# The gate of an mLSTM layer kernel: transposing the normed tokens by VectorE and DRAM instead of TensorE, with the norm's gain in the weights

## The chip, the core and the metric

The kernel runs on one core of a Trainium2 chip, on one layer's worth of work for 2048 tokens of width 1024. The metric is the device time of one execution in microseconds. Engines are named as in the profile: PE (TensorE), DVE (VectorE), ACT (ScalarE), POOL (GpSimd), SP (SyncE, which only issues DMAs here).

## What is computed

One layer: an mLSTM mixer, a squared-ReLU MLP, and then a last part, the only one that the change touches:

```python
h = h + mlstm_mixer(rmsnorm(h, norm_mix), ...)
h = h + sqrelu_mlp(rmsnorm(h, norm_mlp), w1, w2)
gate = jax.nn.sigmoid(rmsnorm(h, norm_ple) @ ple_gate_w + ple_gate_b)   # 1024 x 1024
h = h + gate * (p @ ple_w)                                            # p: 2048 x 256
return rmsnorm(h, norm_final)
```

`rmsnorm(x, g)` is `x * rsqrt(mean(x^2) + eps) * g`, all in float32.

## The kernel before

Products are made on TensorE with both operands split into a high and a low part (`split`, L165: an ACT cast to the high part, a DVE subtract for the low one), so that each product takes three matmuls (`mm3`). A matmul contracts over partitions, so the activations have to stand with their 1024 features on partitions: they are transposed before each product.

**The down projection** of the MLP is a sequence of jobs (`down`, 48 of them). Each ends in 512 KB stores `h_d<-o` (L1287) that POOL issues and that add to the residual stream in DRAM (`h1_d`). Other work is hung on jobs as `side` lists; the table `late` (L1636) hangs the loads and splits of the last part's weights on jobs 41 to 47: eight 128x1024 slices of the gate's weights (`wgt`), two of `ple_w` (`wpl`).

**The last part** takes 16 token tiles of 128 (class `Tok`, loop from L1648). For a tile: `load` brings the 512 KB of `h2` to SBUF; `norm` squares and sums on ACT, makes `r = rsqrt(...)` in a few tiny steps (`rstd`), and multiplies `h2` by `r` and by the broadcast row `row_ple` on DVE into `xs`; `tr0` and `tr1` transpose four 128x128 blocks each on TensorE into the one PSUM bank that `ps_s` gives for `pt`, and `split` reads that bank; `half(0)` and `half(1)` each do 24 matmuls into `pg` (`gate`) and 6 into `pl` (`p @ ple_w`, with `p` transposed earlier), then DVE adds the bias (`g<-pg`), ACT takes the sigmoid, DVE multiplies with `pl` and adds to `h`; `fin` applies the final norm and POOL stores the tile (`out<-h`). The steps of a tile are interleaved with those of its neighbours: while tile t is multiplied, tile t+1 is transposed and tile t+2 normed; `load` of tile t+4 is called in tile t.

Two helpers that were there before are used by the change. `shuffle` (L335) makes a transpose without TensorE: for one 256-feature slice `m` and four token tiles, DVE transposes 32x32 blocks (four `y<-raw` of 128x256), and POOL writes the result to DRAM in four 128 KB DMAs (L341) whose addresses put the blocks where the full transpose wants them. `shuffled` (L344) loads it back as `z`, 128 partitions by 2 x 512. Before, this is done for `p` (class `Early_p`) and in earlier stages.

Buffers come from tagged pools: `Ht` is the large pool of 4 KB rows, `Ot` has 7 buffers (`NO = 7`), used for the `o` tiles of the down projection and for `h2` from tile 2 on. What the program issues is put in its order on each engine by a scheduler, which follows the program's order but moves instructions by its estimates of time; every engine then takes its own queue in order.

Of the kernel before, what the change touches and what calls it, by code (L numbers as in the profile page):

```python
# [8 lines left out]
F32 = mybir.dt.float32  # L9
F32R = mybir.dt.float32r  # L10
AF = mybir.ActivationFunctionType
ALU = mybir.AluOpType
# [4 lines left out]
P = 128  # L17
S = 2048
D = 1024
KD = D // P  # L20
NC = S // P
# [14 lines left out]
def hybrid_mlstm_kernel(  # L36
# [100 lines left out]
    gains = {nm: const.tile([P, KD], F32, name=f"g_{nm}") for nm in ("mix", "hn")}  # L137

    def gain_load(nm, g):
        SP.dma_start(gains[nm], g.rearrange("(k p) -> p k", p=P))  # L140
# [9 lines left out]
    h1_d = dram.tile([NC, P, D], F32, name="h1_d")  # L150
# [18 lines left out]
    def rstd(ss, n):  # L169
# [9 lines left out]
        V.tensor_tensor(y, y, t, op=ALU.mult)  # L179
        return y  # L180

    def small(nm, bufs=3):
        return sb.tile([P, 8], F32, tag=nm, bufs=bufs, name=nm)
# [6 lines left out]
    class Weight:  # L190
# [11 lines left out]
                SP.dma_start(self.st[..., at:at + n], src)  # L202
                at += n

        def prep(self, eng=None):
            self.hi = Ht("whi", self.shape, F32R)
            self.lo = Ht("wlo", self.shape, F32R)
            split(self.hi, self.lo, self.st, eng)
            self.st = None

    def cols_w(w, c0, n=P):
# [2 lines left out]
    def rows_w(w, r0):  # L214
        return Weight(w[r0:r0 + P, :], [P, D])
# [119 lines left out]
    def shuffle(dst, m, srcs, tile_=Ht):  # L335

        y = tile_("y", [P, 8, 4, 32])
        for j in range(4):
            V.transpose(y[:, :, j, :], srcs[j].rearrange("p (b i) -> p b i", i=32))
        for q in range(4):  # L340
            G.dma_start(dst[8 * m:8 * m + 8, :, q].rearrange("b i e -> i b e"),  # L341
                        y[32 * q:32 * q + 32].rearrange("i b j t -> i b (j t)"))

    def shuffled(src, m, tile_=Ht):  # L344
        z = tile_("z", [P, 2, 512])
        SP.dma_start(z, src[8 * m:8 * m + 8].rearrange("(k b) i q e -> (b i) k (q e)", b=4))
        return z
# [4 lines left out]
    def by_quad(d, t):  # L352

        q = t % 4
        return d[t - q:t - q + 4, 32 * q:32 * q + 32]

    class Early(Prep):
# [575 lines left out]
    class Chunk:  # L933
        Cf = Cs = None

        ss, nss = None, H
# [370 lines left out]
    wgt = [rows_w(gate_w, k * P) for k in range(KD)]  # L1307
# [4 lines left out]
    def ple_rows(d, t):  # L1312
        return d[t] if t < NC // 2 else by_quad(d, t)

    class Early_p:
# [21 lines left out]
        def split(self):  # L1337
            self.hi, self.lo = Ht("pTh", [P, 2, 512], F32R), Ht("pTl", [P, 2, 512], F32R)
            split(self.hi, self.lo, self.z)

    class Tok:
        def __init__(self, t, pt):
            self.t, self.pt = t, pt

        def load(self):
            self.h2 = (Ht if self.t < 2 else Ot)("h2", [P, D])
            SP.dma_start(self.h2, ple_rows(h1_d, self.t))

        def norm(self):
            xs, ss = Ht("xs", [P, D]), small("ss1")  # L1350
            A.activation(xs, self.h2, AF.Square, scale=1.0 / 32.0, accum_out=ss[:, 0:1])
            r = rstd(ss[:, :1], 1)
            V.scalar_tensor_tensor(xs, self.h2, r[:, 0:1], rowc["ple"], op0=ALU.mult, op1=ALU.mult)
            self.xs = xs

        def tr(self, i):
            if i == 0:
                self.hi, self.lo = Ht("xTh", [P, KD, P], F32R), Ht("xTl", [P, KD, P], F32R)
            pt, ks = ps_s("pt"), slice(4 * i, 4 * i + 4)
            for k in range(4):  # L1360
                TE.transpose(pt[:, k * P:(k + 1) * P], self.xs[:, (4 * i + k) * P:(4 * i + k + 1) * P], ident)
# [10 lines left out]
        def half(self, n, gate=True):  # L1372

            if n == 0:
                self.ss = small("ssf")
            if gate:
                self.gate(n)
            sl, pg = slice(n * 512, (n + 1) * 512), self.pg
            tk = slice((self.t % 4) * P, (self.t % 4 + 1) * P)
            pl = ps_tr("pl")  # L1380
            for k in range(2):
                mm3(pl, self.pt.hi[:, k, tk], self.pt.lo[:, k, tk], wpl[k].hi[:, sl], wpl[k].lo[:, sl], k == 0, k == 1)
            g, h = St("g", [P, 512]), self.h2[:, sl]
# [91 lines left out]
    for n, pr in ((0, pa[0][0]), (2, pa[0][1])):  # L1475
        e = pr.early()
# [17 lines left out]
    t0, t1 = pa[0][0].trs(), pa[0][1].gets()  # L1494
# [121 lines left out]
    n = ENTER[-1] + NQ  # L1616
    down = [down_job(s % NQ, [pr for pr, e in zip(pairs, ENTER) if e <= s < e + NQ], (x0 if s % NQ < 4 else x1).rows)
            for s in range(n)]
# [10 lines left out]
        up[1][-1].side += pr.preps()  # L1629

    pp = [Early_p(t) for t in (0, 4, 8, 12)]
    toks = [Tok(t, pp[t // 4]) for t in range(NC)]
    for g in range(4):
        down[16 + 4 * g].side.append(pp[g].dma)
        down[18 + 4 * g].side.append(pp[g].put)
    late = {41: [wgt[0].dma, wgt[1].dma, lambda: row_load("ple", norm_ple[0])],  # L1636
            42: [wgt[0].prep, wgt[1].prep, wgt[2].dma, toks[0].load],
            43: [wgt[2].prep, wgt[3].dma, wgt[4].dma, toks[1].load, toks[0].norm],
            44: [wgt[3].prep, wgt[4].prep, wgt[5].dma, toks[2].load, lambda: row_load("gb", gate_b[0])],
            45: [wgt[5].prep, wgt[6].dma, wgt[7].dma, pp[0].get, toks[1].norm, toks[3].load],  # L1640
            46: [wgt[6].prep, wgt[7].prep, toks[0].tr0, pp[0].split],
            47: [wpl[0].dma, wpl[1].dma, toks[0].tr1, lambda: row_load("nf", norm_final)]}
    for s, fs in late.items():
        down[s].side += fs
    run7(up[0] + up[1] + down)


    for t in range(NC):  # L1648
        nx = toks[t + 1] if t + 1 < NC else None
        if nx:  # L1650
            nx.tr0()
        if t == 0:
            toks[t].gate(0)
            pg0 = toks[t].pg
# [11 lines left out]
        if t % 4 == 2 and t + 2 < NC:  # L1666
            pp[t // 4 + 1].split()
        if t % 4 == 0 and t + 4 < NC:
            pp[t // 4 + 1].get()
# [30 lines left out]
```

## Time and profile before

| | |
|---|---|
| Median of 3 runs | 2424.86 us (2423.91 to 2424.92) |
| The profiled execution | 2426.04 us, of which its span is 2424.3 us |
| TensorE busy in the span | 2375.9 us (98%) |
| VectorE, ScalarE, GpSimd busy | 65%, 48%, 25% |
| Start of the last part (first matmul into `pg`) | 2166.9 us |
| DMA share in 2150 to 2175, 2175 to 2200, 2200 to 2225 | 0.91, 0.68, 0.21 |

The span is what the trace covers; the profiled execution's own time is 1.74 us longer. In the rows of the profile, `out<-in` names the tiles that an instruction writes and reads, "L100" is a wrapper through which all engine calls go, so the names tell the groups apart. "Idle before" is the time that the engine stood still just ahead of these instructions, followed by what ended it. "SPq" and "POOLq" are the queues in which SP and POOL issue DMAs.

### The profile page before, as it was taken

The numbers are of one execution on the slowest core, as the hardware profiler recorded it, in microseconds if no ns is written. First come the engines' busy times: TensorE is split into PE (matmuls) and PEld (weight loads), VectorE is DVE, ScalarE is ACT, GpSimd is POOL, SyncE is SP. The second block draws the span as 40 slices with busy tenths as digits, with TensorE's granted clock in tenths as the row PEclk, the third lists the DMA queues.
The fourth block names the chain that finished last, engine by engine and source line by source line (L and its number), as shares of the span: only waits on it lengthen the run. The fifth ranks groups of instructions, "written<-read, shape, count | busy, mean of one in ns | idle before, by whom it ended". The sixth has DMA issues, their size and how long they took to land.

```text
span 2424.3 us, 31650 instructions
## 1 busy us (share of the span) xinstructions
PE 2375.9 (98%) x11317; PEld 1958.0 (81%) x11317; DVE 1573.3 (65%) x2601; ACT 1163.7 (48%) x2166; POOL 601.8 (25%) x633
## 2 busy tenths in 40 slices
PE   7999999999999999999999999999999999999998
PEld 6988888787889987888888888787887888887776
DVE  6667545557777887667674444866676767656665
ACT  5245424436788874433343333544443444445554
POOL 1041122124333324446543333011111111110000
PEclk9999999999999999999999999999999999999999
DMA  5676656867768873457573321667677776892211
GB/s 171 230 214 203 190 143 221 288 220 279 239 218 287 287 261 116 133 160 224 193 233 114 110 96 61 185 148 165 153 184 173 175 161 156 192 229 86 78 56 48
DMA packets 264501, 429.11 MB, mean 177 GB/s; under 512 B 46952, under 2 KB 174312, under 8 KB 264344
## 3 DMA queue, kind: packets, MB, share of 16 engines
q1 hardware_dynamic: 204376, 303.23, 38.2%
q0 software_dynamic: 59680, 123.35, 21.8%
q8 instruction: 88, 1.44, 0.2%
q14 instruction: 69, 0.57, 0.1%
q10 hardware_dynamic: 288, 0.52, 0.1%
HBM read 257.62 MB, written 169.21 MB: 176 GB/s over the span
## 4 chain that ended last, share of the span: by engine, by line
PE 77%; issue 8%; DVE 6%; DMA 4%; ACT 4%; POOL 1%; SPq 0%; DVEq 0%; ACTq 0%; POOLq 0%
PE pa L100 30%; PE pb L100 15%; PE pc L100 7%; PE psf L100 6%; PE pso L100 5%; PE pg L100 4%; PE psv L100 4%; PE pn L100 3%; PE pu L100 1%; PE pt L100 1%; PE pl L100 1%; ACT L100 1%; DMA hst<-hid_d 1%; DMA cb_d<-Clo 1%; DVE h L100 1%
## 5 line engine op out<-in xcount | busy, mean ns | idle before, releaser
L100 PE MATMUL pa<-op 128*128 128x512 f32 x3360 | 826.1, 395 | 6.6 <-ACT e L100 3.6
L100 PEld LDWEIGHTS pa<-op 128*128 128x128 f32 x3360 | 630.4, 188 | 159.0 <-ACT e L100 6.5
L100 PE MATMUL pb<-op 128*128 128x512 f32 x1632 | 407.8, 394 | 0.8 <-DVE op L100 0.8
L100 PEld LDWEIGHTS pb<-op 128*128 128x128 f32 x1632 | 306.2, 188 | 74.0 <-DVE op L100 1.1
L100 DVE TENSOR_TENSOR op<-sa,op 128x1024 fp32r<-128x1024 f32 (+2 forms) x176 | 188.7, 1078 | 147.4 <-ACT op L100 111.6
L100 ACT CAST op<-sa 128x1024 fp32r<-128x1024 f32 (+2 forms) x176 | 156.4, 895 | 167.6 <-PE pb L100 84.2
L1287 POOL DMA_DIRECT2D h_d<-o x96 | 93.1, 973 | 563.3 <-DVE o L100 494.1
L100 ACT COPY e<-pa 128x512 f32<-128x512 f32 x160 | 93.8, 587 | 262.1 <-PE pa L100 261.4
L100 PE MATMUL pc<-op 128*128 128x512 f32 x768 | 191.8, 394 | 0.1
L100 PEld LDWEIGHTS pc<-op 128*128 128x128 f32 x768 | 144.2, 188 | 34.5 <-DVE op L100 0.6
L100 PE MATMUL psv<-whi,xT 128*128 128x272 f32 (+2 forms) x720 | 161.7, 318 | 0.6 <-DVE xT L98 0.6
L100 PE MATMUL psf<-xT,whi 128*128 128x512 f32 x512 | 160.6, 394 | 0.0
L100 DVE TENSOR_TENSOR op<-wst,op 128x512 fp32r<-128x512 f32 x112 | 123.8, 1108 | 34.8 <-ACT op L100 22.0
L100 ACT CAST op<-wst 128x512 fp32r<-128x512 f32 x112 | 92.6, 834 | 108.5 <-DVE op L100 59.6
L100 PEld LDWEIGHTS psv<-whi,xT 128*128 128x128 f32 x720 | 118.9, 189 | 10.0 <-DVE xT L98 0.8
L461 POOL TENSOR_TENSOR sa<-wst 128x512 f32<-128x512 f32 x32 | 58.9, 1841 | 264.8 <-PE pb L100 168.5
L100 PE MATMUL psv<-wlo,xT 128*128 128x272 f32 (+2 forms) x360 | 114.1, 317 | 0.0
L100 PEld LDWEIGHTS psf<-xT,whi 128*128 128x128 f32 x512 | 95.2, 188 | 21.3
L100 PE MATMUL pso<-whi,hThi 128*128 128x512 f32 x256 | 102.1, 400 | 3.7 <-ACT nt L100 2.5
L100 PE MATMUL pg<-whi,xTl 128*128 128x512 f32 x256 | 101.9, 398 | 0.0
L100 PE MATMUL pg<-whi,xTh 128*128 128x512 f32 x256 | 101.1, 395 | 0.0
L100 PE MATMUL pg<-wlo,xTh 128*128 128x512 f32 x256 | 101.0, 394 | 0.0
(254 smaller groups left out, 4338.3 us busy)
## 6 DMA issues: line engine op xcount, KB each, us to landing
wst<-in_mlp_w SPq DMA_DIRECT2D x96, 512.0 KB
h_d<-o POOLq DMA_DIRECT2D x96, 512.0 KB, 12.4
hid_d<-e SPq DMA_DIRECT2D x128, 256.0 KB
hst<-hid_d SPq DMA_DIRECT2D x64, 384.0 KB
wst<-in_mlstm_w_in SPq DMA_DIRECT2D x44, 512.0 KB
vst<-v_d SPq DMA_DIRECT2D x31, 512.0 KB
raw<-in_x SPq DMA_DIRECT2D x16, 512.0 KB
kq<-kq_d SPq DMA_DIRECT2D x16, 512.0 KB
```

The lines of the kernel that those rows point to most:

```text
L100: r = f(*a, **kw)
L461: eng.tensor_tensor(s[:, 0], r1[:, :, P:], r2[:, :, P:], op=add_)
L1287: G.dma_start(rows(h1_d, 2 * q + i), o[i], accum_op=add_)
```

## The change

Four things are done.

- The gain `norm_ple` goes into the gate's weights: `prep` takes a gain per partition, ACT scales while it casts, DVE scales while it subtracts. The row `row_ple` is not loaded any more; a column version `g_ple` (128 x 8) is, by `gain_load`.
- The factor `r` of the norm is applied behind the matmul: `g = pg * r + gb` in one DVE instruction. `norm` now only makes `r`; nothing has to be normed before it is transposed.
- Tiles 0 to 3 transpose the raw `h2` on TensorE, as `xs` before.
- Tiles 4 to 15 are transposed by `shuffle` and `shuffled`, four tiles at a time (class `Early_h`): four more 512 KB loads of the same rows (`raw`, from the 7 buffers of `Ot`), 16 DVE transposes, 16 POOL stores of 128 KB, four `z` loads of 512 KB on SP. `STEPS` spreads this over the four tiles before. `tr` of these tiles is then a split of four 128x256 pieces from SBUF, with nothing on TensorE.

```diff
+    class Early_h:
+        def load(self):
+            self.raw = []
+            for j in range(4):
+                t = Ot("raw", [P, D])
+                SP.dma_start(t, by_quad(h1_d, self.t0 + j) if self.t0 < NC // 2 else h1_d[self.t0 + j])
+                self.raw.append(t)
+        def put(self, m):
+            shuffle(self.d, m, [r[:, m * 256:(m + 1) * 256] for r in self.raw])
+        def get(self, m):
+            self.z[m] = shuffled(self.d, m)
...
         def norm(self):
-            xs, ss = Ht("xs", [P, D]), small("ss1")
-            A.activation(xs, self.h2, AF.Square, scale=1.0 / 32.0, accum_out=ss[:, 0:1])
-            r = rstd(ss[:, :1], 1)
-            V.scalar_tensor_tensor(xs, self.h2, r[:, 0:1], rowc["ple"], op0=ALU.mult, op1=ALU.mult)
+            ss, self.r = small("ss1"), small("rt", 4)[:, 0:1]
+            A.activation(Ht("jn", [P, D]), self.h2, AF.Square, scale=1.0 / 32.0, accum_out=ss[:, 0:1])
+            rstd(ss[:, :1], 1, self.r)
...
         def tr(self, i):
+            if self.e:
+                tk = slice((self.t % 4) * P, (self.t % 4 + 1) * P)
+                for m in (2 * i, 2 * i + 1):
+                    split(self.hi[:, 2 * m:2 * m + 2], self.lo[:, 2 * m:2 * m + 2], self.e.z[m][:, :, tk])
+                return
...
-            V.tensor_tensor(g, pg, rowc["gb"][:, sl], op=ALU.add)
+            V.scalar_tensor_tensor(g, pg, self.r, rowc["gb"][:, sl], op0=ALU.mult, op1=ALU.add)
...
+    gp = [lambda k=k: wgt[k].prep(None, gains["ple"][:, k:k + 1]) for k in range(KD)]
-    late = {41: [wgt[0].dma, wgt[1].dma, lambda: row_load("ple", norm_ple[0])],
-            42: [wgt[0].prep, wgt[1].prep, wgt[2].dma, toks[0].load],
+    late = {41: [wgt[0].dma, wgt[1].dma],
+            42: [gp[0], gp[1], wgt[2].dma, toks[0].load],
...
+    down[30].side.append(lambda: gain_load("ple", norm_ple[0]))
+    STEPS = [[lambda e: e.load(), lambda e: e.put(0)], [lambda e, m=m: e.put(m) for m in (1, 2, 3)],
+             [lambda e, m=m: e.get(m) for m in range(4)], []]
...
+        g, i = t // 4 + 1, t % 4
...
+        if g < 4:
+            for f in STEPS[i]:
+                f(eh[g])
```

(`e` is None for tiles 0 to 3, so `tr` is there as before but reads `h2` instead of `xs`.)

The scheduler moves instructions by this. Three places matter for what follows. A row is an instruction with what it waits for: DMASW and DMAHW are DMAs issued by POOL and by SP or ACT; a name with _49 is that engine's or queue's semaphore.

On SP, where the down projection ends, before: loads of tiles 4 to 8 (`h_19155` and on), with a load of `p` among them.

```order
L1347 DMA h_19155<-h_d 128x1024 [waits DMASW7_49,DMAHW3_49,DMASW6_49,DMASW5_49]
L346 DMA z<-p_d 128x2x512 [waits DMAHW4_49,PE_49]
L1347 DMA h_19235<-h_d 128x1024 [waits DMAHW5_49,DMASW6_49,DMASW1_49]
L1347 DMA h_19358<-h_d 128x1024 [waits DMASW7_49,DMASW2_49]
L1347 DMA h_19485<-h_d 128x1024 [waits DMASW3_49,DMAHW7_49,DMASW0_49,DVE_49]
L1347 DMA h_19608<-h_d 128x1x1024 [waits DMASW4_49,DMAHW0_49,DMASW1_49,Activation_49]
L346 DMA z<-p_d 128x2x512 [waits DMAHW4_49,DMAHW1_49,DVE_49]
```

And after, from the load of tile 4 (`h_19158`) on, the same stretch of SP's queue:

```order
L1373 DMA h_19158<-h_d 128x1024 [waits DMASW7_49,DMAHW3_49,DMASW6_49,DMASW5_49]
L1358 DMA raw<-h_d 128x1x1024 [waits DMAHW4_49,DMASW6_49,DMASW1_49]
L1358 DMA raw<-h_d 128x1x1024 [waits DMAHW5_49,DMASW7_49,DMASW2_49]
L352 DMA z<-p_d 128x2x512 [waits PE_49]
L1358 DMA raw<-h_d 128x1x1024 [waits DMASW3_49,DMAHW7_49,DMASW0_49,DVE_49]
L1358 DMA raw<-h_d 128x1x1024 [waits DMASW4_49,DMAHW0_49,DMASW1_49,Activation_49]
L1373 DMA h_19255<-h_d 128x1024 [waits DMAHW4_49,DMAHW1_49,DVE_49]
L1373 DMA h_19405<-h_d 128x1024 [waits DMAHW5_49,DMAHW2_49,DVE_49]
L1373 DMA h_19537<-h_d 128x1024 [waits DMAHW7_49,DMAHW3_49,DVE_49]
```

The four `raw` loads of the first group stand where the loads of tiles 5 to 8 stood, with the same waits for POOL's stores (DMASW); tiles 5 to 8 come behind them. For the second group, SP's rows are

```order
L1358 DMA raw<-h_d 128x1024 [waits DMASW4_49,DMAHW2_49,DVE_49,Activation_49]
L1358 DMA raw<-h_d 128x1024 [waits DMAHW3_49,DMAHW2_49,DVE_49]
L1358 DMA raw<-h_d 128x1024 [waits DMAHW4_49,DMAHW3_49,DVE_49]
L1358 DMA raw<-h_d 128x1024 [waits DMAHW5_49,DMASW5_49,Activation_49]
L1373 DMA h_19790<-h_d 128x1x1024 [waits DMAHW6_49,DMAHW4_49,DVE_49]
```

in which the second and the third `raw` wait for DVE, which frees the buffer that they take, and for the `raw` load ahead of them in it.

On DVE, in the first token tiles, before (the first row is the split of `ple_w`, `xTl<-pt` at the end is the split of the first transposes of tile 2):

```order
L100 TENSOR_TENSOR wlo<-wst,whi 128x1024 [waits DMAHW0_49,Activation_49]
L100 TENSOR_TENSOR wlo<-wst,whi 128x1024 [waits DMAHW1_49,Activation_49]
L100 TENSOR_SCALAR rsa<-ss_19173 128x1 [waits Activation_49]
L100 TENSOR_TENSOR g<-pg,row_gb 128x512 [waits PE_49]
L100 TENSOR_TENSOR xTl<-pt,xTh 128x512 [waits Activation_49]
L100 TENSOR_TENSOR g<-pg,row_gb 128x512 [waits PE_49]
L100 TENSOR_TENSOR g<-pl,g 128x512 [waits PE_49,Activation_49]
...
L100 SCALAR_TENSOR_TENSOR xs<-h_18774,rsy,row_ple 128x1024 [waits DMAHW3_49,DVE_49]
L100 TENSOR_TENSOR ssf<-ssf 128x1 [waits Activation_49]
L100 TENSOR_SCALAR rsa<-ssf 128x1 [waits DVE_49]
L100 TENSOR_TENSOR xTl<-pt,xTh 128x512 [waits Activation_49]
```

and after:

```order
L100 TENSOR_TENSOR wlo<-wst,whi 128x1024 [waits DMAHW1_49,Activation_49]
L100 STREAM_TRANSPOSE y<-raw 128x8x32 [waits DMAHW4_49]
L100 TENSOR_SCALAR rsa<-ss_19175 128x1 [waits Activation_49]
L100 SCALAR_TENSOR_TENSOR g<-pg,rt,row_gb 128x512 [waits PE_49]
L100 STREAM_TRANSPOSE y<-raw 128x8x32 [waits DMAHW5_49]
L100 TENSOR_TENSOR xTl<-pt,xTh 128x512 [waits Activation_49]
L100 STREAM_TRANSPOSE y<-raw 128x8x32 [waits DMAHW7_49]
L100 STREAM_TRANSPOSE y<-raw 128x8x32 [waits DMAHW0_49]
L100 SCALAR_TENSOR_TENSOR g<-pg,rt,row_gb 128x512 [waits PE_49]
...
L100 TENSOR_TENSOR rst<-rsa,rsy 128x1 [waits Activation_49]
L100 TENSOR_TENSOR xTl<-pt,xTh 128x512 [waits Activation_49]
```

The first `y<-raw` of the four raw tiles, each behind the landing of its load, now stand among the bias adds `g<-pg` of tile 0 and ahead of the last row, the split of tile 2's first transposes; the product into `xs` is gone.

On PE, the second group of transposes of tile 2, before:

```order
L100 MATMUL pl<-whi,pTh 128x512
L100 MATMUL pl<-wlo,pTh 128x512
L100 MATMUL pl<-whi,pTl 128x512
L100 MATMUL pt<-ident,xs 128x128 [waits DVE_49]
L100 MATMUL pt<-ident,xs 128x128 x3
L100 MATMUL pg<-whi,xTh 128x512
L100 MATMUL pg<-wlo,xTh 128x512
```

and after:

```order
L100 MATMUL pl<-whi,pTh 128x512
L100 MATMUL pl<-wlo,pTh 128x512
L100 MATMUL pl<-whi,pTl 128x512
L100 MATMUL pt<-ident,h_18777 128x128 [waits DVE_49]
L100 MATMUL pt<-ident,h_18777 128x128 x3
L100 MATMUL pg<-whi,xTh 128x512
L100 MATMUL pg<-wlo,xTh 128x512
```

Both wait for DVE, that is for the split that reads the bank before; behind them in both stand the 24 matmuls into `pg` of the second half of tile 1. From tile 4 on, the order after has no transposes on PE, and 48 matmuls into `pg` and 12 into `pl` for each tile, as before.

More of the change, by code (lines that the diff above doesn't have):

```diff
@@ L136, in hybrid_mlstm_kernel @@
     G.memset(ones, 1.0)
-    gains = {nm: const.tile([P, KD], F32, name=f"g_{nm}") for nm in ("mix", "hn")}
+    gains = {nm: const.tile([P, KD], F32, name=f"g_{nm}") for nm in ("mix", "hn", "ple")}
     def gain_load(nm, g):
@@ L167, in split, with rstd @@
         (eng or V).tensor_tensor(lo, src, hi.bitcast(F32), op=ALU.subtract)
-    def rstd(ss, n):
+    def rstd(ss, n, out=None):
         T = lambda nm: sb.tile([P, 8], F32, tag=nm, bufs=3, name=nm)[:, :n]
@@ L178, in rstd @@
         V.tensor_scalar(t, t, -0.5, 1.5, op0=ALU.mult, op1=ALU.add)
-        V.tensor_tensor(y, y, t, op=ALU.mult)
-        return y
+        out = y if out is None else out
+        V.tensor_tensor(out, y, t, op=ALU.mult)
+        return out
     def small(nm, bufs=3):
@@ L203, in dma, with prep @@
                 at += n
-        def prep(self, eng=None):
+        def prep(self, eng=None, gain=None):
             self.hi = Ht("whi", self.shape, F32R)
             self.lo = Ht("wlo", self.shape, F32R)
-            split(self.hi, self.lo, self.st, eng)
+            if gain is None:
+                split(self.hi, self.lo, self.st, eng)
+            else:
+                A.activation(self.hi, self.st, AF.Copy, scale=gain)
+                V.scalar_tensor_tensor(self.lo, self.st, gain, self.hi.bitcast(F32), op0=ALU.mult, op1=ALU.subtract)
             self.st = None
@@ L1339, in split, with __init__ @@
             split(self.hi, self.lo, self.z)
+    class Early_h:
+        def __init__(self, t0):
+            self.t0, self.z = t0, {}
+            self.d = dram.tile([32, 32, 4, P], F32, name=f"h2{t0}_d")
+        def load(self):
[8 more added lines that the diff above has]
+            self.z[m] = shuffled(self.d, m)
     class Tok:
-        def __init__(self, t, pt):
-            self.t, self.pt = t, pt
+        def __init__(self, t, pt, e):
+            self.t, self.pt, self.e = t, pt, e
         def load(self):
@@ L1349, in norm @@
         def norm(self):
-            xs, ss = Ht("xs", [P, D]), small("ss1")
-            A.activation(xs, self.h2, AF.Square, scale=1.0 / 32.0, accum_out=ss[:, 0:1])
-            r = rstd(ss[:, :1], 1)
-            V.scalar_tensor_tensor(xs, self.h2, r[:, 0:1], rowc["ple"], op0=ALU.mult, op1=ALU.mult)
-            self.xs = xs
+            ss, self.r = small("ss1"), small("rt", 4)[:, 0:1]
+            A.activation(Ht("jn", [P, D]), self.h2, AF.Square, scale=1.0 / 32.0, accum_out=ss[:, 0:1])
+            rstd(ss[:, :1], 1, self.r)
         def tr(self, i):
@@ L1358, in tr @@
                 self.hi, self.lo = Ht("xTh", [P, KD, P], F32R), Ht("xTl", [P, KD, P], F32R)
+            if self.e:
[3 more added lines that the diff above has]
+                return
             pt, ks = ps_s("pt"), slice(4 * i, 4 * i + 4)
             for k in range(4):
-                TE.transpose(pt[:, k * P:(k + 1) * P], self.xs[:, (4 * i + k) * P:(4 * i + k + 1) * P], ident)
+                TE.transpose(pt[:, k * P:(k + 1) * P], self.h2[:, (4 * i + k) * P:(4 * i + k + 1) * P], ident)
             split(self.hi[:, ks], self.lo[:, ks], pt.rearrange("p (k t) -> p k t", t=P))
@@ L1631, in hybrid_mlstm_kernel @@
     pp = [Early_p(t) for t in (0, 4, 8, 12)]
-    toks = [Tok(t, pp[t // 4]) for t in range(NC)]
+    eh = [None] + [Early_h(t) for t in (4, 8, 12)]
+    toks = [Tok(t, pp[t // 4], eh[t // 4]) for t in range(NC)]
+    gp = [lambda k=k: wgt[k].prep(None, gains["ple"][:, k:k + 1]) for k in range(KD)]
     for g in range(4):
@@ L1635, in hybrid_mlstm_kernel @@
         down[18 + 4 * g].side.append(pp[g].put)
-    late = {41: [wgt[0].dma, wgt[1].dma, lambda: row_load("ple", norm_ple[0])],
-            42: [wgt[0].prep, wgt[1].prep, wgt[2].dma, toks[0].load],
[L1638 to L1641, printed above, removed]
+    late = {41: [wgt[0].dma, wgt[1].dma],
+            42: [gp[0], gp[1], wgt[2].dma, toks[0].load],
+            43: [gp[2], wgt[3].dma, wgt[4].dma, toks[1].load, toks[0].norm],
+            44: [gp[3], gp[4], wgt[5].dma, toks[2].load, lambda: row_load("gb", gate_b[0])],
+            45: [gp[5], wgt[6].dma, wgt[7].dma, pp[0].get, toks[1].norm, toks[3].load],
+            46: [gp[6], gp[7], toks[0].tr0, pp[0].split],
             47: [wpl[0].dma, wpl[1].dma, toks[0].tr1, lambda: row_load("nf", norm_final)]}
+    down[30].side.append(lambda: gain_load("ple", norm_ple[0]))
     for s, fs in late.items():
@@ L1665, in hybrid_mlstm_kernel @@
             nx.tr1()
[L1666 to L1669, printed above, removed]
+        if i == 2 and t + 2 < NC:
+            pp[g].split()
+        if i == 0 and t + 4 < NC:
+            pp[g].get()
         if t == 0:
```

## The prediction

> **What bounds the kernel now.** I read the page first, then the windows of the last part, then its groups, and last the timeline around the first four token tiles.
>
> ```profile
> PE 2375.9 (98%) x11317; PEld 1958.0 (81%) x11317; DVE 1573.3 (65%) x2601; ACT 1163.7 (48%) x2166; POOL 601.8 (25%) x633
> ```
>
> The columns of the next rows are the stretch, its length, busy time of PE, PEld, DVE, ACT and POOL (with instructions), the granted TensorE clock, the DMA share and GB/s.
>
> ```profile
> 2175.00:2200.00 25.00, 24.42 (x112) 19.63 (x111) 12.46 (x23) 14.44 (x24) 1.07 (x1) 1.00 0.68 190
> 2200.00:2225.00 25.00, 24.70 (x113) 19.53 (x111) 17.37 (x39) 13.25 (x27) 1.20 (x2) 1.00 0.21 76
> 2225.00:2250.00 25.00, 24.84 (x114) 19.86 (x113) 13.91 (x34) 14.61 (x31) 0.53 (x1) 1.00 0.12 43
> ```
>
> ```profile
> 2200.67:2215.81 15.14, 14.98 (x69) 11.90 (x68) 10.28 (x23) 8.81 (x17) 0.62 (x1) 1.00 0.17 55
> 2215.81:2230.95 15.14, 15.00 (x69) 11.89 (x68) 9.13 (x22) 7.98 (x16) 0.58 (x1) 1.00 0.17 66
> ```
>
> TensorE is the bound in the last part too: 24.4 to 24.8 us of every 25 at full clock, while VectorE has 8 to 12 us of every 25 free, ScalarE 10 to 12. From 2200 on the DMA engines have four fifths of their time free; before that, at the hand-over from the down projection, they are 0.68 busy. The second table takes one token tile at a time (from one `g<-pg` of a second half to the next): 15.14 us each. So whatever leaves TensorE's queue is worth its time, if nothing else makes TensorE wait.
>
> **What the removal is worth.** Three `g<-pg` adds near the end, of the first halves of tiles 14 and 15 and of the second half of tile 15, give the price of a tile (48 matmuls into `pg`, 12 into `pl`) with transposes, and of half a tile without any, as tile 15 has no successor to transpose:
>
> ```profile
> 2389.70 0.68 DVE L100 TENSOR_TENSOR g<-pg,row_gb 128x512 f32<-128x512 f32 x1
> 2404.73 0.69 DVE L100 TENSOR_TENSOR g<-pg,row_gb 128x512 f32<-128x512 f32 x1 [1.71 <-PE pg L100]
> 2411.67 0.69 DVE L100 TENSOR_TENSOR g<-pg,row_gb 128x512 f32<-128x512 f32 x1 [4.05 <-PE pg L100]
> ```
>
> 2411.67 - 2404.73 = 6.94 us for 30 matmuls, so 13.88 us for a tile without transposes, against 15.14 (15.03 in the last full tile, from the first two rows): the eight transposes cost TensorE 1.26 us with the gaps around them. Twelve tiles lose them (4 to 15): **12 x 1.26 = 15.1 us**, all of it on the path.
>
> The Trainium skill (VectorE: DVE Perf Modes, "The three transpose paths") gives 390 ns for a 128x128 transpose on TensorE and 311 ns on VectorE, in 32x32 blocks only, and its rules prefer TensorE where PSUM will do as destination. With its 390 ns the eight would be 3.1 us and the twelve tiles 37 us (an estimate from that page); the trace's 1.26 us a tile decides, and my sum has 15.1.
>
> **What the other engines get instead.** Groups of the last part (busy us, mean ns, idle before):
>
> ```profile
> L100 DVE TENSOR_TENSOR g<-pl,g 128x512 f32<-128x512 f32 x32 | 22.1, 692 | 29.8 <-ACT g L100 22.9 <-PE pl L100 7.0
> L100 DVE TENSOR_TENSOR xTl<-pt,xTh 128x512 fp32r<-128x512 f32 x32 | 22.0, 686 | 12.4 <-ACT xTh L100 12.4
> L100 DVE SCALAR_TENSOR_TENSOR xs<-h,rsy,row_ple 128x1024 f32<-128x1024 f32 x16 | 20.6, 1284 | 0.8 <-DVE rsy L100 0.3
> L100 ACT ACTIVATE g<-g 128x512 f32<-128x512 f32 x32 | 20.1, 632 | 44.2 <-DVE g L100 44.0
> L100 PE MATMUL pt<-ident,xs 128*128 128x128 f32 x128 | 19.7, 276 | 2.8 <-DVE xs L100 1.8 <-DVE ssf L100 0.6
> L100 ACT CAST xTh<-pt 128x512 fp32r<-128x512 f32 x32 | 18.6, 580 | 55.5 <-PE pt L100 55.4
> ```
>
> and the same kinds of instruction that the change adds, where they stand elsewhere in this kernel:
>
> ```profile
> L100 DVE STREAM_TRANSPOSE y<-raw x64: 391/403/447, 158.6 to 1111.0; 128x256 f32<-128x256 f32 x64
> L100 DVE TENSOR_TENSOR op<-hst,op 128x256 fp32r<-128x256 f32 x8 | 3.3, 417 | 0.0
> L100 ACT CAST op<-hst 128x256 fp32r<-128x256 f32 x8 | 3.3, 407 | 9.5 <-PE pb L100 8.2 <-DVE op L100 1.2
> mlp_d<-y POOLq DMA_DIRECT2D x32, 128.0 KB, 4.5
> out<-h POOLq DMA_DIRECT2D x14, 512.0 KB, 3.8
> ```
>
> VectorE loses per tile one `xs` product and two `xTl` subtracts (1.28 + 1.37 = 2.65 us) and gains four 128x256 subtracts and four 32x32 transposes (1.67 + 1.61 = 3.28): 9.13 to 10.28 becomes 9.8 to 10.9 of 13.88 us. ScalarE swaps two casts of 580 ns for four of 407: 8.4 to 9.3 of 13.88. Both stay under TensorE, so they cost nothing while their queue is not blocked. At tiles 8 and 12 the first split stands behind the table load of the tile before, and TensorE covers that with `pl` matmuls drawn ahead; I put 0.5 us for the two together. The eight weight casts with a gain are one instruction each as before; the only thing that TensorE can notice of them is tile 0, whose second transposes now have, by the order, 30 matmuls between them and the first where they had 42, and so less cover for the split before: 0 to 2 us, of which I take 0.5. The broadcast load of the norm's row goes, and the tiny `g_ple` load goes into SP's queue near the start, behind loads of its own kind:
>
> ```profile
> 13.31 3.68 SPq L140 DMA_DIRECT2D g_hn<-in_mlstm_head_norm  x1
> 22.32 6.34 SPq L558 DMA_DIRECT2D v_d<-ev  x2
> 39.43 0.88 ACT L100 CAST whi<-wst 128x816 fp32r<-128x816 f32 x1
> ```
>
> It moves two `v_d` stores and seven weight loads back by at most 3.7 us. Two stores that span 6.3 us are a queue that waits for its data, and the first cast of such a weight comes 11 us after them. That cover hides the load: nothing; without it, 3.7 us.
>
> **Where it costs: tiles 0 to 3.** Group 1's four raw loads take the places in SP's queue, and the buffers, of the loads of tiles 5 to 8. These were held back until the last accumulating stores of the down projection landed. SP's rows, POOL's rows, and the landing of those two stores:
>
> ```profile
> 2178.11 0.32 SPq L1347 DMA_DIRECT2D h<-h_d  x1
> 2182.30 0.32 SPq L1347 DMA_DIRECT2D h<-h_d  x1
> 2192.84 0.32 SPq L1347 DMA_DIRECT2D h<-h_d  x1
> 2195.41 0.57 SPq L1347 DMA_DIRECT2D h<-h_d  x1
> ```
>
> ```profile
> 2172.19 1.06 POOL L1287 DMA_DIRECT2D h_d<-o  x1 [8.23 <-DVE o L100]
> 2179.31 1.07 POOL L1287 DMA_DIRECT2D h_d<-o  x1 [6.05 <-ACT o L100]
> ```
>
> ```profile
> h_d<-o POOLq DMA_DIRECT2D x1, 512.0 KB, 20.6
> h_d<-o POOLq DMA_DIRECT2D x1, 512.0 KB, 16.0
> SPq L1347 <- DMA h_d<-o: 24.1, 5, 10.1
> ```
>
> 2172.19 + 20.6 = 2192.8 and 2179.31 + 16.0 = 2195.3: those are the two starts on SP. Before, nobody hurried for these loads. Now VectorE's order has `y<-raw` of the third and fourth raw tile ahead of the second `g<-pg` of tile 0 and of the `xTl` of tile 2's first transposes. There is one PSUM bank for `pt`, so TensorE's second four transposes of tile 2 wait for that `xTl`, and the 24 `pg` matmuls of tile 1's second half are queued behind them. Before, TensorE stood at these places only so long:
>
> ```profile
> 2190.50 0.63 PE L100 MATMUL pt<-ident,xs 128*128 128x128 f32 x4 [0.58 <-DVE ssf L100]
> 2194.45 0.60 PE L100 MATMUL pt<-ident,xs 128*128 128x128 f32 x4
> ```
>
> Without that 0.58 us TensorE comes to the second group at 2193.9. The changed order puts the last `o` copy of the down projection ahead of the two `ple_w` casts, so the second accumulating store may be issued up to 7 us earlier; it shares the DMA engines with the first and I put both landings at 2191.5 and 2193.5 (bounds 2189 and 2195.4). The fourth raw load then lands 3.3 us later (an estimate, 512 KB in 3.8 us is the nearest row), at 2196.8. From there VectorE and ScalarE work in a chain: `y` 0.40, `g` 0.69, sigmoid 0.63, table load, two small activations, square, cast 0.58, `xTl` 0.69.
>
> ```profile
> L100 ACT ACT_TABLE_LOAD x32 | 41.1, 1283 | 0.6
> L100 ACT ACTIVATE rsy<-rsa 128x1 f32<-128x1 f32 x32 | 6.3, 197 | 3.2 <-DVE rsa L100 3.0
> L100 ACT ACTIVATE g<-h 128x512 f32<-128x512 f32 x32 | 19.9, 623 | 8.5 <-DVE h L100 8.5
> ```
>
> With 1.28 + 2 x 0.20 + 0.62 that is 5.3 us, so TensorE goes on at 2202.1: **a stall of 8.2 us** (3.5 with the early bound and an instant landing, 11 with 2195.4 and 3.8 us to land). 0.6 us more falls at tile 3's transposes, whose `xTl` has eleven more `y<-raw` ahead of it, and the old 0.58 us goes.
>
> The Trainium skill (Perfetto Trace Analysis, "Tensor Engine Instruction") says that ScalarE, VectorE and GpSimd are strictly first in, first out, and TensorE nearly so; if VectorE could pass over a `y<-raw` that waits, the stall would be nothing. No row of before shows a ready instruction overtaking a waiting one.
>
> The sum: -15.1 + 8.2 + 0.6 - 0.6 + 0.5 + 0.5 = **-5.9 us**. The profiled execution took 2424.3 in its span and 1.74 around it, 2426.04; the median of the three runs is 2424.86. The difference goes on the median: **2419.0 us**. Some 0.2%, 4.85 us, is what a measurement of this kernel can tell from no change.
>
> **The rivals.** (a) *The raw tiles come in time.* For it: the accumulating stores wait for each other more than for data, and with the earlier `o` copy the second may land with the first. Against it: even at 2189 for the last load the chain reaches into TensorE's time by 3.5 us. Then -15.1 + 1 to 4: 2410 to 2414. Chance 0.17.
>
> (b) *Groups 2 and 3 come late: slower.* Their raw tiles find few free buffers (seven for all): the first takes the buffer of tile 2 (6 for the next group) once its output has landed, the second and the third the first's, one after the other, and POOL's `y` stores stand behind an output. Three rounds of a 3.8 us load and four transposes that VectorE fits into half a tile (6.9 us), 32 us; with the output before (about 4), the `y` stores behind (4.5 to 7.4) and the `z` load (3.8), `z` is there about 46 us after tile 3's end, and needed after four tiles, 55.5 us. Every microsecond over 55.5 stops TensorE at tile 8 and again at tile 12. From 61 us on, with each round 5 us longer, the kernel is slower than before by more than the bound (-5.9 + 2 x 5.4 = 4.9); at 64 it gives 2436. Against it: 9 us of slack by my count, and a DMA share of 0.12 to 0.21. Chance 0.17.
>
> (c) *The hand-over costs all of it.* The fourth raw tile lands at 2200 as the DMA engines are still busy, TensorE waits 11 us or more, some 2 us are lost again at tiles 8 and 12: -15.1 + 11 + 3 to 5, 2423 to 2427. Chance 0.18.
>
> **How the numbers follow.** The forecast itself, a stall of 5 to 11 us, gives 2416 to 2422 and has 0.48. About 0.7 of it is below 2420.0 (2424.86 - 4.85): with (a) that is 0.34 + 0.17 = 0.51 faster. Same: 0.14 from the forecast, 0.14 from (c) and 0.04 from (b), 0.32. Slower: 0.17, most of (b) and the end of (c). The range from 2410 to 2428 leaves out what lies far in (b), and little below.
>
> **What would show it.** Right: `pt` groups only for tiles 0 to 3, a tile's `g<-pg` 13.88 us apart from tile 4 on, and one idle stretch of TensorE of about 8 us near 2194, ended by VectorE's `xTl`, with VectorE in its turn waiting for `raw<-h_d` and SP for `h_d<-o`. Wrong: no such stretch (a), idle time of some microseconds before the first `pg` of tiles 8 and 12 with ScalarE waiting for `z<-h_d` (b), or tiles that stay at 15 us because VectorE's queue is late at each.

## The result, and the profile after

| | before | after |
|---|---|---|
| Median | 2424.39 us (4 runs, 2423.1 to 2424.92) | 2441.86 us (4 runs, 2440.31 to 2447.22) |
| Profiled execution | 2426.04 us | 2447.22 us |
| Span | 2424.3 us | 2445.5 us |

The changed kernel is slower: ratio 1.0077, 95% interval 1.0059 to 1.0094. Forecast was 2419.0, between 2410 and 2428.

The profiled execution of after is the slowest of its four. It was already 5.2 us late at a store of the down projection (POOL's `h_d<-o` at 2111.62 us, 2106.44 before and 2106.53 in h4_only, whose code is the same up to there), ahead of all that matters here; so of the 21.2 us between the two spans, 16.0 belong to the last part.

The same windows as before, in the profile after (the stretch, its length, busy time of PE, PEld, DVE, ACT, POOL, the granted TensorE clock, DMA share, GB/s):

```profile
2175.00:2200.00 25.00, 16.87 (x78) 13.41 (x76) 5.08 (x8) 6.60 (x9) 2.17 (x2) 0.90 0.79 205
2200.00:2225.00 25.00, 17.64 (x61) 14.08 (x62) 12.86 (x33) 8.06 (x16) 8.12 (x14) 0.76 0.39 110
2225.00:2250.00 25.00, 25.00 (x114) 20.32 (x113) 12.90 (x29) 13.81 (x28) 1.75 (x3) 1.00 0.76 229
2300.00:2325.00 25.00, 21.77 (x81) 16.82 (x80) 11.57 (x34) 11.46 (x26) 2.97 (x6) 0.86 0.67 209
```

The first two rows hold the hand-over: 15.5 us without work on TensorE, and a granted clock of 0.90 and 0.76, where it was 1.00 throughout before. The last row holds tile 8. The waits of TensorE in the last part, with the total, the count and the longest:

```profile
PE pt L100 <- DVE xTl L100: 15.5, 2, 9.4
PE pg L100 <- ACT xTh L100: 6.3, 4, 3.2
```

The two stops at the transposes, on TensorE and on VectorE:

```profile
2201.24 1.11 PE L100 MATMUL pt<-ident,h 128*128 128x128 f32 x4 [9.36 <-DVE xTl L100]
2216.81 1.11 PE L100 MATMUL pt<-ident,h 128*128 128x128 f32 x4 [6.13 <-DVE xTl L100]
```

```profile
2195.19 0.45 DVE L100 STREAM_TRANSPOSE y<-raw 128x256 f32<-128x256 f32 x1 [6.71 <-DMA raw<-h_d]
2200.16 0.45 DVE L100 STREAM_TRANSPOSE y<-raw 128x256 f32<-128x256 f32 x1 [3.83 <-DMA raw<-h_d]
2200.53 0.65 DVE L100 TENSOR_TENSOR xTl<-pt,xTh 128x512 fp32r<-128x512 f32 x1
2206.53 0.45 DVE L100 STREAM_TRANSPOSE y<-raw 128x256 f32<-128x256 f32 x1 [5.35 <-DMA raw<-h_d]
2211.60 0.45 DVE L100 STREAM_TRANSPOSE y<-raw 128x256 f32<-128x256 f32 x1 [4.62 <-DMA raw<-h_d]
```

The eight groups of transposes in the trace are those of tiles 0 to 3 in turn, so 2201.24 is the first group of tile 2 and 2216.81 its second. VectorE stands at each `y<-raw` until that raw tile lands, and only then splits the transposes that TensorE needs out of the bank. The mechanism of the forecast is there, but at two places, and the raw tiles land much later than their loads are issued. SP's rows for them:

```profile
2185.07 0.57 SPq L1358 DMA_DIRECT2D raw<-h_d  x1
2187.88 0.54 SPq L1358 DMA_DIRECT2D raw<-h_d  x1
2192.48 0.52 SPq L1358 DMA_DIRECT2D raw<-h_d  x1
2195.03 0.53 SPq L1358 DMA_DIRECT2D raw<-h_d  x1
```

From issue to landing that is 10.1, 12.3, 14.1 and 16.6 us, and the tiles land 5.0, 6.4 and 5.1 us apart. What the DMA engines do meanwhile:

```profile
2195.00:2200.00 5.00, 0.00 (x0) 0.00 (x0) 1.14 (x3) 0.63 (x1) 0.00 (x0) 0.50 0.27 106
2200.00:2206.00 6.00, 4.76 (x15) 3.95 (x16) 1.02 (x2) 0.00 (x0) 0.00 (x0) 0.56 0.26 104
```

They are not busy: a quarter of them moves 105 GB/s and three quarters stand still, with nothing else to do. 512 KB at 105 GB/s are 5.0 us, the distance of the landings. The four raw loads of the first group (`by_quad`: four blocks of 32 rows from four tiles in DRAM, 4 x 32 x 1024) behave as if each used 4 of the 16 engines, the same ones, one after the other. The trace also keeps the times at which a load's semaphore was raised: once about 1 us after the issue and four times as it lands (2193.75 to 2195.16 for the first) for each of these loads, sixteen times for each of the 32-row DMAs that replace them in raw4 below. The first load has a second reason to be late: from 2185 to 2192 the DMA engines were busy all the time, with the accumulating stores among others.

```profile
2185.00:2192.00 7.00, 6.87 (x30) 5.25 (x28) 1.23 (x1) 3.85 (x5) 0.00 (x0) 1.00 0.99 254
```

The Trainium skill says just this (DMA: Bandwidth & Descriptors, "Why a DMA increments its semaphore by 16 and not by 1"): the number of engines is the largest up to 16 that divides the slowest dimension that is not 1, of both sides, and a smaller number takes the lowest engines. With 4 as the outermost size that is 4 of 16; the share of 0.26 and the four late raises agree.

The clock is the second thing. In the trace after, behind the 6.13 us of stillness and at tile 8 behind 3.23 us, where ScalarE waits for `z`:

```profile
2216.50:2222.00 5.50, 5.19 (x15) 4.21 (x16) 5.25 (x20) 3.05 (x7) 3.35 (x6) 0.50 0.39 66
2318.00:2324.00 6.00, 5.49 (x13) 4.38 (x14) 4.55 (x17) 5.11 (x15) 0.55 (x1) 0.50 0.37 147
```

```profile
2318.05 0.40 ACT L100 CAST xTh<-z 128x256 fp32r<-128x256 f32 x1 [4.65 <-DMA z<-h_d]
```

At 0.50 the matmuls start 0.43 us apart in place of 0.23, for 4 to 6 us, so each of these three stops cost 2 to 3 us more than its own length. Before, no stop in the last part was over 0.58 us. The Trainium skill has this rule too (TensorE: Matmul & The Clock Gate, "Part 1: The HAM clock gate"): half the clock after an idle window of about 3.4 us, and again full after about as long under work. Here 3.23 us were enough, and 2.02 us at tile 12 were not. In the runs below the clock also fell behind shorter stops, of 1.85 us (h4_only), 1.93 (late4), 2.33 (raw4) and 2.40 (fill), and not behind 1.86 (raw4_h4): the length of a stop alone does not tell, and the page's figure is no safe bound here. Behind the stop of late4, which a second one of 1.04 us follows:

```profile
2350.00:2356.00 6.00, 4.96 (x13) 3.48 (x12) 4.18 (x17) 6.00 (x19) 0.00 (x0) 0.51 0.16 55
```

### The profile page after: what moved, and what is told of

It reads as the page before. It is cut to its first block, busy times and chain, and to the rows that moved or that the text cites. A ratio compares the mean times of both kernels' runs of the same rounds, so it can differ in the third digit from the quotient of the medians.

```text
span 2445.5 us, 31660 instructions
## 1 busy us (share of the span) xinstructions
PE 2377.0 (97%) x11221; PEld 1960.2 (80%) x11221; DVE 1572.8 (64%) x2657; ACT 1165.7 (48%) x2190; POOL 629.7 (26%) x681
## 4 chain that ended last, share of the span: by engine, by line
PE 43%; issue 8%; DMA 6%; DVE 3%; POOL 1%; ACT 1%; SPq 0%; DVEq 0%; ACTq 0%; POOLq 0%
PE pa L100 24%; PE pb L100 12%; PE pc L100 6%; PE pg L100 2%; DVE op L100 1%; DMA raw<-h_d 1%; POOL h_d L1293 1%; DMA h_d<-y 1%; DMA out<-h 1%; DMA hst<-hid_d 1%; DMA h_d<-o 1%; DMA wst<-in_mlp_w 1%; DMA z<-h_d 0%; DVE raw L100 0%; DMA z<-tz_d 0%
```

## The experiments

Two theories stood against each other. *Narrow*: the loss comes from loads of the `by_quad` form, which run on 4 of 16 engines, and from VectorE's queue, whose head waits for them. *Buffers*: the loss comes from when the loads can start, that is from the 7 buffers of `Ot` and the accumulating stores that free them, as the forecast had it. Intervals are those of the ratio to the kernel before.

| run | what differs from the changed kernel | median us | ratio to before |
|---|---|---|---|
| (the changed kernel) | | 2441.86 | 1.0077 (1.0059 to 1.0094) |
| fold_only | all tiles by TensorE | 2422.03 | 0.9982 (0.9972 to 0.9992) |
| no_first | tiles 4 to 7 by TensorE | 2421.71 | 0.9986 (0.9973 to 0.9999) |
| raw4 | raw loads wide | 2432.48 | 1.0027 (1.0018 to 1.0037) |
| h4_only | `h2` loads wide | 2432.96 | 1.0035 (1.0022 to 1.0048) |
| raw4_h4 | both wide | 2421.29 | 0.9986 (0.9976 to 0.9996) |
| late_h4 | `h2` loads wide, transposes of raw later | 2427.30 | 1.0003 (0.9993 to 1.0014) |
| late4 | both wide, transposes of raw later | 2414.23 | 0.9950 (0.9931 to 0.9969) |
| late4_ahead3 | the same, `h2` loaded three tiles ahead | 2412.77 | 0.9948 (0.9930 to 0.9967) |
| before_h4 | kernel before, `h2` loads wide | 2426.41 | 1.0002 (0.9993 to 1.0012) |
| fill | useless matmuls in the second stop | 2443.40 | 1.0072 (1.0054 to 1.0090) |

**One part alone.** In fold_only no tile takes the new route, in no_first the first group does not (the lines of both runs together):

```diff
-    eh = [None] + [Early_h(t) for t in (4, 8, 12)]
+    eh = [None] * 4                                        # fold_only
+    eh = [None, None] + [Early_h(t) for t in (8, 12)]      # no_first
-        if g < 4:
+        if g < 4 and eh[g]:
```

fold_only:

> All 16 token tiles are transposed by TensorE again; only the gain in the weights, the late factor r and the raw h2 as the transposes' input stay of the change. Every theory of the loss that names the loads or the stores of the new route expects no loss here: 2420 to 2425 us, as before or a little below, with no idle stretch of TensorE over 2 us from 2160 us on. The rival that the loss comes from the gain (scaled casts, the g_ple load, the shifted DMA queues) expects over 2430 us.

It took 2422.03 us, 0.18% less than before, with no wait of TensorE's matmuls in the list of waits. The gain in the weights is not the loss; it is a small win by itself. Two `g<-pg` one tile apart show where from:

```profile
2380.44 0.75 DVE L100 SCALAR_TENSOR_TENSOR g<-pg,rt,row_gb 128x512 f32<-128x512 f32 x1 [3.65 <-PE pg L100]
2395.25 0.75 DVE L100 SCALAR_TENSOR_TENSOR g<-pg,rt,row_gb 128x512 f32<-128x512 f32 x1 [3.66 <-PE pg L100]
```

14.81 us for a tile with eight transposes, where it was 15.14. Before, the transposes waited for `xs` in ten places, 1.8 us together, and that is gone; what else is in the 0.33 us is not shown.

no_first:

> Tiles 4 to 7 are transposed by TensorE as well; groups 8 to 11 and 12 to 15 keep the new route. If the loss at the hand-over (9.4 and 6.1 us of idle TensorE and the low clock behind each) belongs to the first group's raw loads, it goes: 8 x 1.26 = 10.1 us saved, 9 to 11 us lost at tiles 8 and 12, so 2421 to 2427 us. If the hand-over is late for another reason, the idle stretches near 2192 and 2211 us stay and the time is over 2435 us.

It took 2421.71 us. The waits of its trace:

```profile
PE pg L100 <- ACT xTh L100: 3.6, 3, 2.7
```

Nothing is left of the stops at the transposes: they belong to the first group's raw loads. What is left is all at tile 12 (the clock is 0.51 in the 6 us behind it) and eats most of the saving of eight tiles: from the second half of tile 11 to that of tile 15, eight half tiles take 62.6 us in place of 55.5.

**The form of the loads.** Each `by_quad` load is issued as four DMAs of 32 rows, first for the raw tiles of the first group (raw4), then also for the `h2` loads of tiles 8 to 15 (raw4_h4), then for those alone (h4_only):

```diff
-                SP.dma_start(t, by_quad(h1_d, self.t0 + j) ...)
+                    for k in range(4):
+                        SP.dma_start(t[32 * k:32 * k + 32], h1_d[self.t0 + k, 32 * j:32 * j + 32])
...
-            SP.dma_start(self.h2, ple_rows(h1_d, self.t))
+                for k in range(4):
+                    SP.dma_start(self.h2[32 * k:32 * k + 32], h1_d[self.t - q + k, 32 * q:32 * q + 32])
```

> The four raw loads of the first group are each issued as four DMAs of 32 rows in place of one DMA over 4 x 32 rows. Theory narrow: the one DMA ran on 4 of the 16 DMA engines (share 0.26, 105 GB/s, 5 us each, one behind the other); now each lands within 4 us of its issue, idle time of TensorE at the hand-over falls from 15.5 to under 5 us, and the time to 2424 to 2432 us. Theory buffers (the step of the prediction): the loads still start at 2185, 2188, 2192 and 2195 us as buffers come free; the stall stays at 6 us or more and the time at 2432 to 2440 us. The scheduler also puts some of the transposes of raw later in VectorE's queue here, which helps under both.

> As the run with raw in four DMAs, and the h2 loads of tiles 8 to 15, which have the same form, in four DMAs each too. Theory narrow: those loads stand in front of the z loads of tiles 8 and 12 on four DMA engines; without them z lands earlier, TensorE's idle time and low clock there (6.8 and 4.3 us over the pace) shrink by half or more, 3 to 7 us less than the run with raw alone. If z is late because POOL's stores of y and the buffers are late, no difference (within 2 us).

> The changed kernel with only the h2 loads of tiles 8 to 15 in four DMAs each; the raw loads of the first group stay one narrow DMA each, and VectorE's order is that of the changed kernel. Theory narrow: the hand-over is as bad as before (9 and 6 us of idle TensorE at the two groups of tile 2), and the stops at tiles 8 and 12 shrink, by about the 11 us that the same edit gave on top of wide raw loads or less: 2431 to 2437 us. If the h2 loads have nothing to do with those stops, 2440 to 2444 us.

raw4 took 2432.48 us, 9.4 less than the changed kernel; by its time alone it lies on the border of the two theories. Its waits:

```profile
PE pg L100 <- ACT xTh L100: 8.6, 2, 6.3
PE pt L100 <- DVE xTl L100: 4.4, 1, 4.4
```

At the hand-over 4.4 us are left of 15.5, as narrow has it (under 5); the gain does not all arrive, because TensorE now waits longer for `z` at tiles 8 and 12 (8.6 us in place of 6.3). But this does not yet speak for the width of the loads, because the scheduler also changed VectorE's order, as the expectation says. The first `xTl` of these rows, the split ahead of tile 2's first transposes, stood behind two `y<-raw` in the changed kernel and now stands ahead of them all; the second stood behind four and now stands behind one:

```profile
2182.93 0.68 DVE L100 TENSOR_TENSOR xTl<-pt,xTh 128x512 fp32r<-128x512 f32 x1
2191.11 0.45 DVE L100 STREAM_TRANSPOSE y<-raw 128x256 f32<-128x256 f32 x1 [7.50 <-DMA raw<-h_d]
2195.58 0.69 DVE L100 TENSOR_TENSOR xTl<-pt,xTh 128x512 fp32r<-128x512 f32 x1 [0.31 <-ACT xTh L100]
```

So the first stop, of 9.4 us, went by the order. The first raw tile comes no sooner as four DMAs: they were issued from 2178.67 to 2182.69, as buffers came free, and it landed at 2191.11, not "within 4 us"; the narrow load of h4_only, issued at 2179.66, landed at 2189.89. The width shows at the last tiles: by their semaphores the four raw tiles of raw4 had landed at 2197.3, while the fourth narrow one of h4_only landed at 2206.4. raw4_h4 took another 11.2 us off, more than the 3 to 7 expected, and its waits are

```profile
PE pt L100 <- DVE xTl L100: 3.7, 1, 3.7
PE pg L100 <- ACT xTh L100: 3.6, 2, 1.9
```

h4_only took 2432.96 us, with the hand-over as bad as in the changed kernel and tiles 8 and 12 mended:

```profile
PE pt L100 <- DVE xTl L100: 14.3, 2, 9.0
PE pg L100 <- ACT xTh L100: 1.9, 1, 1.9
```

So one edit, with the order that comes with it, acts on the one place and the other on the other: 9.4 and 8.9 us alone, 20.6 together. The `h2` loads matter though nobody waits for them: they stand ahead of the `z` loads in SP's queue, and four DMA engines still work on them when the `z` loads come. In the changed kernel, the semaphore of the `z` load issued at 2302.32 was raised twelve times by 2306.87 and the last four times from 2315.74 to 2318.03, where ScalarE's cast of tile 8 begins; the narrow `h2` load issued ahead of it, at 2298.46, landed from 2313.75 to 2316.86. In h4_only all sixteen raises of a `z` load issued at 2293.43 fall between 2297.53 and 2299.45. While TensorE stood before tile 8:

```profile
2316.00:2319.00 3.00, 0.49 (x1) 0.50 (x2) 0.43 (x1) 0.40 (x1) 0.00 (x0) 0.81 0.26 99
```

The kernel before has the same loads of tiles 8 to 15. With four DMAs each in it (before_h4):

> The kernel before, with the h2 loads of tiles 8 to 15 in four DMAs of 32 rows each. Theory narrow: in the kernel before nobody waits for these loads, so nothing changes: 2422 to 2427 us, ratio within 0.15% of 1. If narrow loads cost by themselves, it is 3 us or more faster.

2426.41 us, no difference: there the narrow loads cost nothing, as nobody waits for them or for what stands behind them.

**The place in VectorE's queue.** The transposes of the first group's raw tiles are called in the second tile, not in the first and the second; by the order they then stand behind the split of tile 2's first transposes (late_h4 with narrow raw loads, late4 with wide ones):

```diff
+    LATE = [[lambda e: e.load()], [lambda e, m=m: e.put(m) for m in range(4)],
+            [lambda e, m=m: e.get(m) for m in range(4)], []]
...
-            for f in STEPS[i]:
+            for f in (LATE if g == 1 else STEPS)[i]:
```

> As the run with wide h2 loads alone, narrow raw loads, and the first group's transposes of raw called one tile later: they now stand behind the split of tile 2's first transposes and ahead of that of its second. Theory queue head: the two stops at tile 2 go, and one takes their place at tile 3's first transposes, from about 2206 to 2218 us (the fourth raw lands near 2211.6, then twelve transposes of 0.4 us and a split); idle of TensorE at the hand-over 10 to 13 us in one piece in place of 15.5 in two, 3 to 6 us less than the run with wide h2 loads alone. If the place in VectorE's queue does not matter, the stops stay where they were.

> As the run with raw and h2 in four DMAs each, and the first group's transposes of raw on VectorE are called one tile later, so that none of them stands ahead of the split of tile 2's first transposes. Theory queue head: the 3.7 us of idle TensorE at the second transposes of tile 2 and the 2 us of low clock behind it go, about 5 us less than 2421.3: 2415 to 2418 us; what is left is at tiles 8 and 12. If the stall there is not made by VectorE's queue, it stays, and the time is 2419 us or more.

late_h4 took 2427.30 us, 5.7 less than h4_only, and the stops moved as expected, to one at tile 3's first transposes:

```profile
2213.61 1.11 PE L100 MATMUL pt<-ident,h 128*128 128x128 f32 x4 [12.63 <-DVE xTl L100]
```

The loads start within 0.7 us of those of h4_only; VectorE's order decides at which split the wait for them is paid. late4 took 2414.23 us, 7.1 less than raw4_h4 and a little under the 2415 to 2418 expected, and of TensorE's waits only those for `z` are left, both at tile 12:

```profile
PE pg L100 <- ACT xTh L100: 3.0, 2, 1.9
```

Between late_h4 and late4 lie 13.1 us. Part of it is the width: in late_h4 VectorE gets the fourth raw tile at 2207.24, in late4 it had landed at 2198.0 by its semaphores. But the order differs here too: sixteen `y<-raw` stand ahead of the split that stops TensorE in late_h4, eight ahead of the same split in late4. No run has wide raw loads in the changed kernel's order, so the share of the width at the hand-over stays open.

**Buffers, in tiles 8 and 12.** late4 with `h2` loaded three tiles ahead (`toks[t + 3].load()` in place of `t + 4`), so that the raw tiles of groups 2 and 3 find one more buffer:

> As the run before it, and h2 is loaded three tiles ahead in place of four, which leaves one more of the seven buffers to the raw tiles of groups 2 and 3. If z is late at tiles 8 and 12 because of the buffers, idle time of TensorE before tiles 8 and 12 goes from 3.6 us to under 1.5 and the time is 2 to 6 us lower than without it (2411 to 2415 us). If it is late because POOL's stores of y stand behind outputs and behind each other, it stays within 2 us.

2412.77 us (2411.05 to 2416.87) against 2414.23 (2413.11 to 2415.65): the runs overlap, so the time does not tell. The wait for `z` fell from 3.0 to 1.6 us in the profiled execution, not quite to the 1.5 expected. What holds `z` back there by the rest, buffers or POOL's stores, stays open. This is the lowest median of all runs, 0.52% under the kernel before, but not clear of late4.

**The clock.** 30 matmuls of no use stand ahead of tile 2's second transposes (their bank is never read; nothing else is changed):

```diff
+        if t == 1:
+            dm = ps_mm("dm")
+            for k in range(30):
+                TE.matmul(dm, toks[1].hi[:, k % KD], wgt[k % KD].hi[:, :512], start=k == 0, stop=k == 29)
         if nx and t > 0:
             nx.tr1()
```

> The changed kernel as it is, with 30 matmuls of no use (their bank is never read, 6.95 us at the usual pace) in TensorE's queue just ahead of the second transposes of tile 2, where it stood still for 9.4 us. Theory clock: the matmuls that follow a stillness of 3 us or more run at 0.43 us in place of 0.23 for 4 to 6 us; with 2 to 3 us of stillness left the slow stretch there goes and the time falls by about 2 us, to 2439 to 2441 us. If the slow stretch has another cause (what VectorE or the DMAs do then), it stays and the time is unchanged or longer.

The expectation placed the stop of 9.4 us there; it is the one of 6.13, so the matmuls filled it whole:

```profile
2208.35 7.09 PE L100 MATMUL dm<-whi,xTh 128*128 128x512 f32 x30
2215.28 0.60 PE L100 MATMUL pt<-ident,h 128*128 128x128 f32 x4
```

```profile
2199.00:2204.00 5.00, 4.85 (x16) 4.02 (x17) 0.09 (x1) 0.00 (x0) 0.00 (x0) 0.60 0.25 102
2215.00:2220.00 5.00, 5.00 (x25) 4.09 (x25) 4.67 (x18) 2.54 (x5) 3.43 (x6) 1.00 0.45 79
```

Behind the first stop, which is as long as before (9.45 us), the clock is down again; behind the filled one it is 1.00, while VectorE and POOL are as busy there as in the changed kernel. So stillness makes the slow stretch. The kernel's time did not fall with it (2443.40 against 2441.86, the runs overlap; 2439 to 2441 was expected): tile 12 waits for `z` longer instead (4.5 us, 3.1 in the changed kernel).

## Why the prediction was wrong

- *The removal, 12 x 1.26 us.* Right in size. From tile 13 on a tile takes 13.88 us (`g<-pg` of the first halves of tiles 14 and 15):

```profile
2411.28 0.75 DVE L100 SCALAR_TENSOR_TENSOR g<-pg,rt,row_gb 128x512 f32<-128x512 f32 x1 [1.04 <-PE pg L100]
2425.16 0.75 DVE L100 SCALAR_TENSOR_TENSOR g<-pg,rt,row_gb 128x512 f32<-128x512 f32 x1 [1.60 <-PE pg L100]
```

  But by fold_only 0.33 us of the 1.26 come with the raw `h2` as input, and 0.93 with the removal of the transposes.
- *VectorE and ScalarE stay under TensorE.* Right: where no load is waited for, TensorE sets the pace. The small terms (g_ple, the scaled casts, tile 0) came to nothing, by fold_only.
- *The stall at the hand-over, 8.2 us.* **This step failed**: "The fourth raw load then lands 3.3 us later". The loads started at 2192.5 and 2195.0 for the third and fourth, 1 to 1.5 us behind the forecast's 2191.5 and 2193.5 in an execution that was 5.2 us late. They landed 14.1 and 16.6 us later. The price was taken from `out<-h`, of the same 512 KB but over 128 rows in one piece, and set below even its 3.8 us without a reason; the raw loads have another form, run on 4 engines, and queue behind each other there. The same step hid a second stop: the first two raw loads, with 2178 and 2182 as starts, seemed to be in time, so the split ahead of tile 2's first transposes, behind the second `y<-raw` in VectorE's order, was not counted. It cost the 9.4 us. These two loads took 10.1 and 12.3 us, and wide loads would not have helped much there: in late4 the first two raw tiles were there at 2191.97 and 2194.39, in late_h4, with narrow ones, at 2190.28 and 2195.43. The DMA engines were busy then (share 0.99 from 2185 to 2192), which the 3.3 us leave out as well. One bound of this step does not follow from its terms either: 2189 with an instant landing and the chain of 5.3 us is 2194.3, a stall of 0.4 us and not 3.5.
- *Nothing behind a stall.* The sum had no term for the clock. Three stops were followed by a slow stretch: it cost about 2 us behind the first, 2.7 behind the second, some 3 at tile 8.
- *Rival (b), z late at tiles 8 and 12.* It happened, with 0.17 of the chances. Its slack of 9 us rested on `z` and raw loads of 3.8 us each, without narrow `h2` loads ahead of them. From the second half of tile 7 to that of tile 11, eight half tiles took 62.3 us (2309.94 to 2372.23) where 8 x 6.94 are 55.5, and the next eight 59.9: 6.8 and 4.3 us over.
- *Rival (c), the hand-over costs all of it.* It came nearest there, with busy DMA engines and a stop of 11 us or more, but it had the fourth raw tile at 2200 and one stop; the tile landed at 2211.6 and there were two.

The sum with the measured terms, in the profiled execution: stops at the hand-over 15.5 - 0.6, slow clock there 2 + 2.7, removal -15.1, tiles 8 and 12 +11.1, together 15.6; the last part lost 16.0. The mechanism forecast for the stall, VectorE's queue, is shown by late_h4 against h4_only and late4 against raw4_h4. That the narrow loads hold `z` back is shown by h4_only and the raises of the semaphores, which also count the four engines. How much of the hand-over is the width of the raw loads and how much VectorE's order stays open, as raw4 changed both.

The trace of before had the row. While tile 8's `h2` load ran there alone:

```profile
2241.00:2244.00 3.00, 3.00 (x14) 2.43 (x13) 1.95 (x4) 2.57 (x6) 0.00 (x0) 1.00 0.25 76
```

a quarter of the engines and 76 GB/s.

## What to carry to other kernels

Price a load by its access pattern, not by its bytes: a DMA whose outermost size is 4 ran at a quarter of the engines, and it delays all that is queued behind it, wide loads too. Before an instruction that waits for a load is put into a shared queue, look at which split, cast or evacuation then stands behind it; one step later in the order was worth 6 to 7 us here. And a stop of TensorE can cost some 1.5 to 3 us on top, here behind all stops of 2.3 us or more and some shorter ones, so two stops are dearer than their lengths.

## What the runs showed of the hardware

- Narrow loads in flight together did not share the idle engines: they landed 5.0 to 6.4 us apart at a DMA share of 0.26. As four DMAs of 32 rows, the first two raw tiles of late4 were there 2.4 us apart:

```profile
2191.97 0.45 DVE L100 STREAM_TRANSPOSE y<-raw 128x256 f32<-128x256 f32 x1 [3.85 <-DMA raw<-h_d]
2194.39 0.45 DVE L100 STREAM_TRANSPOSE y<-raw 128x256 f32<-128x256 f32 x1 [1.55 <-DMA raw<-h_d]
```

- After 9.4, 6.1 and 3.2 us of stillness the granted clock was 0.50, with matmuls of 512 columns 0.43 us apart, for 4 to 6 us; after 2.0 us it was not. In other runs stops of 1.85 to 2.40 us were followed by 0.50 for 3 to 6 us, and others of 1.6 to 1.9 us were not.
